# Four pieces of sample attention in place of eight, and the page loads spread along them

## The chip, the core and the metric

The kernel runs on one core of a Trainium2 chip. The metric is the device time of one execution in microseconds (us), the median of several runs. Engines are named as the profile names them: PE is TensorE's matmul, PEld its weight load, DVE is VectorE, ACT is ScalarE, POOL is GpSimd, SP is SyncE, which here issues every DMA.

## What is computed

One inference step of a decoder of two layers, in fp32, on 256 new prompt tokens and on 8 sample tokens, each sample with 256 cached tokens in two pages of 128. Cut to layer 2, which the change is in:

```
q, k, v, z = split(x @ w_in_attn)            # x: 256 prompt rows and 8 sample rows, width 1024
q, k = rope(q), rope(k)                      # first 32 of each head's 128 columns
prompt:  causal attention of 8 heads over the 256 rows
sample:  rows_k = cache_k[page_table], rows_v = cache_v[page_table]   # 2 pages a sample
         p = softmax(concat(q . rows_k, q . k_new) / sqrt(128))
         o = p @ concat(rows_v, v_new)
y = (o * silu(z)) @ w_out_attn
x = layernorm(sqrt(2) * x + y)
```

Layer 1 is a gated short convolution with projections of the same sizes.

## The kernel before

**Slabs.** Activations lie transposed: 8 blocks of 128 features by 264 columns (256 prompt, 8 sample). Each weight matrix is cut into slabs of 128 output features, numbered 0 to 79; slab 40+i is called "slab i" of layer 2 here, i from 0 to 31 (queries 0 to 7, keys 8 to 15, values 16 to 23, gate 24 to 31). A slab is 512 KB. Every weight is used as a high and a low part: ACT makes `hi` (L113), DVE makes `lo` (L118), and PE runs three matmuls for each of 8 blocks, 24 a slab (L125 to L127, "the stream").

**Order.** The program is written as a table of hooks: `at(n, phase, f)` puts a step in slab n, `begin(n)` runs the phases "dma", "pe", "s0", "hi", "lo", "s1a", "s1b", "s1" and so on in this order, and "peh" runs between a slab's first 12 and last 12 matmuls. Nothing is reordered later: each engine works its own list in order. SP issues the load of a slab's raw weights only behind the `lo` that frees one of four buffers (L116 to L118, then `load`), and the page loads `kv_load` stand in the same list, in phase "dma" of the slab that `KV_AT` names.

**Samples on cached pages.** 32 page tiles of 512 KB (16 of keys, two DMAs each, L242; 16 of values, one DMA each, L245) share 10 buffers `kv`; the first 10 are loaded in layer 1. `qk(step)`, steps 0 to 3, multiplies the samples' queries with four key tiles (16 matmuls, L690, into `sd`); `pvd(step)`, steps 4 to 7, the probabilities with four value tiles (8 matmuls, L742, into `dps`). The chip's trace shows each fp32 matmul as two. `QK_AT` and `PV_AT` name the slabs of these eight pieces. Tile i+10 takes the buffer of tile i, so its load waits for the piece that reads tile i.

**Around it.** PE's results lie in three rotating `acc` buffers; `k_evac` (ACT, L566 and L568) frees them in slabs 9 to 16, phase "s0". Prompt attention of head h: `s_mm` (PE, L622, L623) at the start of slab 16+h, `s_max` (DVE, L631 to L634), `s_exp` (ACT, L640), `s_norm` (DVE, L645, L647), `p_tr` and `v_tr` (PE, L653, L612) in the middle of slab 17+h. `s_mm`, `p_tr`, `v_tr` and `pv` take turns on three `att` buffers. `rope` (DVE, L577 to L580) for the last four key heads stands in slab 16, behind `s_norm` of head 0. After the last piece `od_copy`, `od_tr`, `os_fin` and `g_batch` make the samples' output and gate it; blocks that `g_batch` leaves out get it in `z_evac` by a copy on POOL (L776).

Of the kernel before, what the change touches and what calls it, by code (L numbers as in the profile page):

```python
# [38 lines left out]
C_COS = C_MASK + 128  # L39
C_SIN = C_COS + N  # L40
C_END = C_SIN + N
QK_AT = (6, 7, 10, 11)
KV_AT = (7, 7, 8, 8, 9, 9, 10, 11, 12, 13, 14, 15, 16, 17, 18, 19, 21, 21, 22, 22, 23, 24)
PV_AT = (21, 22, 24, 26)
SWAP = [(j + 16) % 32 for j in range(32)]


def build(tc, a):
    nc = tc.nc
    pe, act, dve, pool, sp = nc.tensor, nc.scalar, nc.vector, nc.gpsimd, nc.sync  # L50

    with ExitStack() as top:
# [79 lines left out]
        def at(n, phase, f, *args):  # L132
            hooks.setdefault((n, phase), []).append(lambda: f(*args))
# [371 lines left out]
        with tc.tile_pool(name="l1", bufs=1) as p1, ExitStack() as late_pool:  # L505
# [301 lines left out]
            S = 40  # L807
# [16 lines left out]
            at(S + 1, "s1", sd_fill)  # L824
            for i, n in enumerate(QK_AT):
                at(S + n, "peh", qk, i)
# [5 lines left out]
            at(S + 20, "s1a", pd_cp)  # L832
            for i, n in zip(range(NKV, 32), KV_AT):
                at(S + n, "dma", kv_load, i // 4, i % 4)
            for i, n in enumerate(PV_AT):
                at(S + n, "pe", pvd, 4 + i)
            at(S + 26, "s1", od_copy)
            at(S + 27, "pe", od_tr)
            at(S + 27, "s1", os_fin)
            at(S + 28, "s1", g_batch, 4)  # L840

            for h in range(8):
                n = S + 16 + h
# [180 lines left out]
```

## Time and profile before

| | |
|---|---|
| runs | 293.76, 291.53, 289.59 us; median 291.53 |
| the profiled execution's own time | 292.53 us |
| its span (first to last instruction) | 290.8 us |
| PE busy | 278.4 us, 96% |
| DVE, ACT, POOL busy | 186.0, 170.0, 62.8 us |
| DMA | 64.01 MB, mean 220 GB/s |

A busy PE is not yet a PE that does useful work at its full pace: its share counts overlapping matmuls. So the place where time is lost is read from the distances between the starts of matmuls, and from what ended PE's idle times. The chain of waits follows the end of the program back, at each step to what released it.

### The profile page before, as it was taken

How to read it: one execution, taken by the hardware profiler on the slowest of the kernel's cores; microseconds unless marked ns; L12 is line 12 of the kernel's file. 1: busy time of each engine (PE TensorE's matmuls, PEld its weight loads, DVE VectorE, ACT ScalarE, POOL GpSimd, SP SyncE). 2: the span in 40 equal slices, each digit the busy share in tenths (PEclk: the TensorE clock that was granted, in tenths of full speed). 3: DMA queues.
4: the chain of work that ended last, by engine and by line, in shares of the span. 5: the costliest groups of instructions: out<-in, count | busy, mean ns of one | idle time of the engine just before them, and what ended most of it. 6: DMA issues, size and time to landing. Idle time of an engine off the chain costs nothing.

```text
span 290.8 us, 6250 instructions
## 1 busy us (share of the span) xinstructions
PE 278.4 (96%) x2345; PEld 261.8 (90%) x2345; DVE 186.0 (64%) x347; ACT 170.0 (58%) x328; POOL 62.8 (22%) x120
## 2 busy tenths in 40 slices
PE   7999999999999999999999999979999999999980
PEld 4999999999999999999979699879779879999970
DVE  2957967465759759659985466796447147746144
ACT  4766655455366556355946399978557535553133
POOL 3110212021010108919420000000000003005643
PEclk9999999999999999999999999999999999999996
DMA  6985979999666763422069997979696643520003
GB/s 196 378 280 180 320 249 338 402 382 381 221 205 235 244 219 129 149 74 73 0 192 323 404 405 275 377 240 321 195 327 195 233 144 96 194 74 1 2 0 149
DMA packets 23215, 64.01 MB, mean 220 GB/s; under 512 B 2834, under 2 KB 5394, under 8 KB 23186
## 3 DMA queue, kind: packets, MB, share of 16 engines
q1 hardware_dynamic: 23186, 63.63, 62.8%
q8 instruction: 18, 0.29, 0.4%
q14 instruction: 11, 0.09, 0.1%
HBM read 60.30 MB, written 3.32 MB: 219 GB/s over the span
## 4 chain that ended last, share of the span: by engine, by line
PE 81%; ACT 7%; DMA 6%; DVE 3%; issue 1%; SPq 1%; DVEq 0%; ACTq 0%
PE acc L125 22%; PE acc L127 22%; PE acc L126 22%; DMA raw<-w 4%; PE dps L742 3%; ACT hi L113 3%; DMA kv<-kc 2%; PE sd L690 1%; PE acc L448 1%; PE o L662 1%; PE acc L449 1%; PE acc L452 1%; PE s L623 1%; PE pt L653 1%; ACT rp L568 1%
## 5 line engine op out<-in xcount | busy, mean ns | idle before, releaser
L118 DVE TENSOR_TENSOR lo<-raw,hi 128x1024 fp32r<-128x1024 f32 (+1 forms) x82 | 98.1, 1204 | 14.2 <-ACT hi L113 13.9
L113 ACT CAST hi<-raw 128x1024 fp32r<-128x1024 f32 (+1 forms) x82 | 82.9, 1017 | 38.8 <-DMA raw<-w 24.4
L125 PE MATMUL acc<-m0h,hi 128*128 128x264 f32 (+1 forms) x344 | 97.6, 284 | 0.0
L127 PE MATMUL acc<-m0h,lo 128*128 128x264 f32 (+1 forms) x344 | 97.5, 283 | 0.0
L126 PE MATMUL acc<-m0l,hi 128*128 128x264 f32 (+1 forms) x344 | 97.4, 283 | 0.0
L125 PE MATMUL acc<-m1h,hi 128*128 128x264 f32 x264 | 76.8, 291 | 0.0
L127 PE MATMUL acc<-m1h,lo 128*128 128x264 f32 x264 | 74.7, 283 | 0.0
L126 PE MATMUL acc<-m1l,hi 128*128 128x264 f32 x264 | 74.6, 283 | 0.0
L125 PEld LDWEIGHTS acc<-m0h,hi 128*128 128x128 f32 x344 | 64.7, 188 | 0.8 <-issue 0.4
L127 PEld LDWEIGHTS acc<-m0h,lo 128*128 128x128 f32 x344 | 64.9, 189 | 0.0
L126 PEld LDWEIGHTS acc<-m0l,hi 128*128 128x128 f32 x344 | 64.7, 188 | 0.0
L125 PEld LDWEIGHTS acc<-m1h,hi 128*128 128x128 f32 x264 | 49.7, 188 | 2.2 <-issue 2.1
L126 PEld LDWEIGHTS acc<-m1l,hi 128*128 128x128 f32 x264 | 49.7, 188 | 0.1
L127 PEld LDWEIGHTS acc<-m1h,lo 128*128 128x128 f32 x264 | 49.7, 188 | 0.0
L404 POOL COPY uo<-up 128x10 f32<-128x10 f32 x8 | 8.0, 1003 | 70.7 <-DVE up L403 62.4
L279 ACT ACTIVATE sqm<-xf 128x264 f32<-128x264 f32 x14 | 5.8, 423 | 20.1 <-DVE xf L259 20.1
L259 DVE SCALAR_TENSOR_TENSOR xf<-xf,acc 128x264 f32<-128x264 f32 x16 | 6.6, 425 | 12.4 <-PE acc L266 10.6
L287 POOL TENSOR_TENSOR q<-q,sqm 128x264 f32<-128x264 f32 x12 | 13.1, 1089 | 1.6 <-ACT sqm L279 1.5
L782 DVE TENSOR_TENSOR gt<-z,q 128x256 f32<-128x256 f32 (+1 forms) x8 | 3.4, 430 | 13.6 <-ACT z L773 13.6
L631 DVE TENSOR_TENSOR s<-s,cst 128x256 f32<-128x256 f32 x8 | 3.4, 431 | 12.3 <-PE s L623 12.3
L602 POOL COPY vs<-vh 128x8 f32<-128x8 f32 x8 | 1.6, 204 | 39.6 <-ACT vh L601 39.6
L286 POOL TENSOR_TENSOR sr<-sr,xf 128x264 f32<-128x264 f32 x10 | 9.3, 928 | 2.3 <-DVE xf L259 2.3
(187 smaller groups left out, 341.8 us busy)
## 6 DMA issues: line engine op xcount, KB each, us to landing
raw<-w SPq DMA_DIRECT2D x76, 512.0 KB, 4.7
kv<-kc SPq DMA_DIRECT2D x32, 256.0 KB, 6.1
kv<-vc SPq DMA_DIRECT2D x16, 512.0 KB, 5.4
raw<-w SPq DMA_DIRECT2D x7, 256.0 KB, 5.8
k_o<-k SPq DMA_DIRECT2D x8, 132.0 KB, 5.0
v_o<-vh SPq DMA_DIRECT2D x8, 132.0 KB, 4.5
y_o<-xf SPq DMA_DIRECT2D x4, 264.0 KB, 2.1
xf<-x SPq DMA_DIRECT2D x3, 264.0 KB, 5.8
```

The source lines that it names most:

```text
L113: act.copy(his[n][sl], raws[n][sl])
L118: dve.tensor_sub(los[n][sl], raws[n][sl], his[n].bitcast(F32)[sl])
L125: pe.matmul(acc, wh, mh[:, k, 0:w], start=first and k == ks[0], stop=False)
L126: pe.matmul(acc, wh, ml[:, k, 0:w], start=False, stop=False)
L127: pe.matmul(acc, wl, mh[:, k, 0:w], start=False, stop=last and k == ks[-1])
L259: dve.scalar_tensor_tensor(x, x, ALPHA, acc, ALU.mult, ALU.add)
L279: act.activation(self.last_sq, xf[:, m], AF.Square)
L286: pool.tensor_tensor(self.sr, self.sr, xf[:, m], ALU.add)
L287: pool.tensor_tensor(self.q, self.q, self.last_sq, ALU.add)
L404: pool.tensor_copy(uo[:, f], up[:, T:N + 2])
L631: dve.tensor_tensor(diag, diag, mask, ALU.add)
L742: pe.matmul(dps[0][32 * j:32 * j + 32, 512 * c:512 * c + 512], pm[b2][pg][:, j, :], kv_tiles[step, j][:, 512 * c:512 * c + 512], start=ste ...
```

## The change

The keys' pieces (`qk`) move from slabs 6, 7, 10, 11 to 7, 7, 14, 14; the values' pieces (`pvd`) from 21, 22, 24, 26 to 22, 22, 27, 27. The 22 page loads of layer 2 stand in other slabs: the first six were two a slab in slabs 7, 8 and 9, and are now two in slab 8 and one each in 9, 10, 11 and 12. The steps behind the last piece stand two slabs later, and the samples' gating takes six blocks in one batch, not four.

```
-QK_AT = (6, 7, 10, 11)
-KV_AT = (7, 7, 8, 8, 9, 9, 10, 11, 12, 13, 14, 15, 16, 17, 18, 19, 21, 21, 22, 22, 23, 24)
-PV_AT = (21, 22, 24, 26)
+QK_AT = (7, 7, 14, 14)
+KV_AT = (8, 8, 9, 10, 11, 12, 13, 14, 15, 15, 16, 17, 18, 19, 20, 21, 23, 23, 24, 24, 25, 25)
+PV_AT = (22, 22, 27, 27)
...
-            at(S + 26, "s1", od_copy)
-            at(S + 27, "pe", od_tr)
-            at(S + 27, "s1", os_fin)
-            at(S + 28, "s1", g_batch, 4)
+            at(S + 28, "s0", od_copy)
+            at(S + 29, "pe", od_tr)
+            at(S + 29, "s1", os_fin)
+            at(S + 30, "s1", g_batch, 6)
```

The first place is SP's list in slabs 6 to 10. `raw52` is slab 12's weights (40 + 12), `kv2_2` the key tile of step 2 and sample pair 2; of a tile's two DMAs one row is shown, and the rows that read a page's number are left out. Before:

```order
L103 DMA raw52_2178<-w 128x1024
L242 DMA kv2_2_2221<-kc 128x512
L242 DMA kv2_3_2224<-kc 128x512
L103 DMA raw53_2238<-w 128x1024
L242 DMA kv3_0_2281<-kc 128x512
L242 DMA kv3_1_2284<-kc 128x512
L103 DMA raw54_2295<-w 128x1024
L242 DMA kv3_2_2331<-kc 128x512
L242 DMA kv3_3_2334<-kc 128x512
L103 DMA raw55_2347<-w 128x1024
L103 DMA raw56_2351<-w 128x1024
L245 DMA kv4_0_2380<-vc 128x1024
```

Now:

```order
L103 DMA raw52_2178<-w 128x1024
L103 DMA raw53_2216<-w 128x1024
L242 DMA kv2_2_2275<-kc 128x512
L242 DMA kv2_3_2278<-kc 128x512
L103 DMA raw54_2289<-w 128x1024
L242 DMA kv3_0_2325<-kc 128x512
L103 DMA raw55_2338<-w 128x1024
L103 DMA raw56_2342<-w 128x1024
L242 DMA kv3_1_2371<-kc 128x512
L103 DMA raw57_2381<-w 128x1024
L103 DMA raw58_2385<-w 128x1024
L242 DMA kv3_2_2420<-kc 128x512
```

Of these page tiles none stands ahead of `raw53`, where there were two, two ahead of `raw54` in place of four, and three ahead of `raw55` in place of six.

The second place is PE's list around the first keys' piece, which was in the middle of slab 6 (weights `hi46`, `lo46`); `kv0_0` to `kv0_3` are the tiles of step 0. Before, the last matmul of the stream ahead of the piece, the piece's first four and the stream's next behind its 16:

```order
L127 MATMUL acc_2180<-m0h_89,lo46_1915 128x266
L690 MATMUL sd_1911<-kv0_0_755,zq_2017 16x256
L690 MATMUL sd_1911<-kv0_1_795,zq_2017 16x256
L690 MATMUL sd_1911<-kv0_2_830,zq_2017 16x256
L690 MATMUL sd_1911<-kv0_3_876,zq_2017 16x256
L125 MATMUL acc_2180<-m0h_89,hi46_1913 128x266
```

Now the last four matmuls of step 0 and the first four of step 1, in the middle of slab 7:

```order
L690 MATMUL sd_1911<-kv0_0_755,zq_2017 16x256
L690 MATMUL sd_1911<-kv0_1_795,zq_2017 16x256
L690 MATMUL sd_1911<-kv0_2_830,zq_2017 16x256
L690 MATMUL sd_1911<-kv0_3_876,zq_2017 16x256
L690 MATMUL sd_1911<-kv1_0_911,zq_2017 16x256
L690 MATMUL sd_1911<-kv1_1_951,zq_2017 16x256
L690 MATMUL sd_1911<-kv1_2_986,zq_2017 16x256
L690 MATMUL sd_1911<-kv1_3_1032,zq_2017 16x256
```

Step 1 now follows step 0 with no matmul of the stream between them.

## Rows read from the trace of the kernel before

**Rows 1.** The page: busy time, share and count of each engine.

```profile
PE 278.4 (96%) x2345; PEld 261.8 (90%) x2345; DVE 186.0 (64%) x347; ACT 170.0 (58%) x328; POOL 62.8 (22%) x120
```

**Rows 2.** Timeline of PE around the keys' piece of slab 6, then the first and the last of 65 matmuls of the undisturbed stream: start in us, duration, engine, line, what it does.

```profile
144.11 0.29 PE L127 MATMUL acc<-m0h,lo 128*128 128x266 f32 x1
144.32 1.92 PE L690 MATMUL sd<-kv,zq 128*16 128x256 f32 x32
146.18 0.39 PE L125 MATMUL acc<-m0h,hi 128*128 128x266 f32 x1
146.40 0.29 PE L126 MATMUL acc<-m0l,hi 128*128 128x266 f32 x1
...
152.11 0.28 PE L126 MATMUL acc<-m1l,hi 128*128 128x264 f32 x1
...
159.82 0.28 PE L127 MATMUL acc<-m1h,lo 128*128 128x264 f32 x1
```

**Rows 3.** Timeline of PE around the values' piece of slab 21, and around the same `s_mm` one slab earlier, where no piece stands ahead of it.

```profile
201.59 0.39 PE L622 MATMUL s<-k,q 128*128 128x128 f32 x2
201.81 0.60 PE L623 MATMUL s<-k,q 128*128 128x256 f32 x2
...
206.24 0.28 PE L127 MATMUL acc<-m1h,lo 128*128 128x264 f32 x1
206.45 1.92 PE L742 MATMUL dps<-kv,pm 128*32 128x512 f32 x16
208.31 0.49 PE L622 MATMUL s<-k,q 128*128 128x128 f32 x2
208.63 0.60 PE L623 MATMUL s<-k,q 128*128 128x256 f32 x2
```

**Rows 4.** Waits of PE by what ended them: us in total, times, longest.

```profile
PE s L622 <- ACT P L640: 1.5, 1, 1.5
PE pt L653 <- DVE P L647: 0.6, 1, 0.6
```

**Rows 5.** Timeline of PE around the keys' piece of slab 11; in brackets the idle time ahead of an instruction and what ended it.

```profile
164.98 0.62 PE L690 MATMUL sd<-kv,zq 128*16 128x256 f32 x6
166.12 1.89 PE L690 MATMUL sd<-kv,zq 128*16 128x256 f32 x26 [0.52 <-DMA kv<-kc]
167.93 0.39 PE L125 MATMUL acc<-m1h,hi 128*128 128x264 f32 x1
```

**Rows 6.** Timeline of PE: end of the stream's first half in slab 17, and `p_tr` of head 0.

```profile
186.58 0.28 PE L127 MATMUL acc<-m1h,lo 128*128 128x264 f32 x1
187.43 0.70 PE L653 MATMUL pt<-cst,P 128*128 128x128 f32 x3 [0.56 <-DVE P L647]
```

**Rows 7.** The chain of waits from 152.5 to 195 us: start, us, what.

```profile
153.42 6.12 DMA kv<-kc
159.61 7.67 DMA raw<-w
...
186.03 0.82 ACT P L640 x4
...
191.52 0.49 PE s L622 x2
```

**Rows 8.** Timeline of ACT in slabs 9 to 11, with the idle time ahead of an instruction; L566 is `k_evac`.

```profile
158.26 1.05 ACT L113 CAST hi<-raw 128x1024 fp32r<-128x1024 f32 x1 [1.67 <-DMA raw<-w]
162.27 1.06 ACT L113 CAST hi<-raw 128x1024 fp32r<-128x1024 f32 x1 [2.97 <-DMA raw<-w]
...
167.35 1.05 ACT L113 CAST hi<-raw 128x1024 fp32r<-128x1024 f32 x1 [2.36 <-DMA raw<-w]
...
169.16 0.38 ACT L566 COPY k<-acc 128x264 f32<-128x264 f32 x1
169.57 0.37 ACT L568 COPY rp<-acc 32x264 f32<-32x264 f32 x1
```

**Rows 9.** Busy time of each engine from 165 to 168 us, granted clock, DMA share and GB/s.

```profile
165.00:168.00 3.00, 2.48 (x34) 1.04 (x33) 1.21 (x3) 0.65 (x1) 0.00 (x0) 1.00 1.02 408
```

**Rows 10.** The page, DMA issues of whole weight slabs: count, KB each, median us from issue to landing.

```profile
raw<-w SPq DMA_DIRECT2D x76, 512.0 KB, 4.7
```

**Rows 11.** Timeline of DVE in slabs 16 and 17, between `s_max` of head 0 and `s_max` of head 1.

```profile
181.91 0.43 DVE L631 TENSOR_TENSOR s<-s,cst 128x256 f32<-128x256 f32 x1 [1.19 <-PE s L623]
...
183.59 1.23 DVE L118 TENSOR_TENSOR lo<-raw,hi 128x1024 fp32r<-128x1024 f32 x1 [0.39 <-ACT hi L113]
...
186.88 0.17 DVE L645 RECIPROCAL mx<-mx 128x2 f32<-128x2 f32 x1 [0.79 <-ACT P L640]
...
190.35 0.17 DVE L634 TENSOR_SCALAR mx<-mx 128x2 f32<-128x2 f32 x1
```

**Rows 12.** The kernel's two ends: timeline of PE from its first matmuls on, and the last stretch by windows (columns as in rows 9; 0.50 is the granted clock).

```profile
0.78 3.57 PE L75 MATMUL warmp<-const-bfloat16-1.0 128*128 128x512 bf16 x8 [0.78 <-PEq L1006]
...
4.67 0.42 PE L448 MATMUL acc<-m0h,w 128*128 128x264 f32 x1
4.89 0.42 PE L449 MATMUL acc<-m0l,w 128*128 128x264 f32 x1
...
7.65 0.28 PE L449 MATMUL acc<-m0l,w 128*128 128x264 f32 x1
...
286.00:290.80 4.80, 0.00 (x0) 0.00 (x0) 1.16 (x3) 0.53 (x2) 0.22 (x1) 0.50 0.57 219
```

## The prediction, made before the changed kernel ran

> **What bounds the kernel now.** I read the page first: PE is busy for 96% of the span [rows 1]. With so full an engine a change can gain only where the starts of its matmuls lie farther apart than the stream's own pitch. That pitch is (159.82 - 152.11) / 64 = 0.1205 us [rows 2], so 24 matmuls, a slab, take 2.9 us. Then I listed PE's waits and, because a wait of a pipelined engine is longer than its idle time, measured each in the timeline. In the stretch of the change there are three: a page that is late in slab 11 [rows 5], `p_tr` in slab 17 and `s_mm` in slab 18 [rows 4]. Last I followed the chain of waits back from that `s_mm`, to see whether the three have one cause.
>
> They mostly do. The chain runs from `s_mm` at 191.52 to ACT's exponential, through ACT's list back to a `hi` at 167.35 [rows 8], from there to a weight load issued at 159.61 that took 7.67 us, and to a page load ahead of it that took 6.12 us [rows 7]. The queue is full there: 408 GB/s [rows 9], by which a tile or slab of 512 KB [rows 10] takes 524,288 / 408e9 = 1.29 us. In slabs 7, 8 and 9 SP issues two page tiles and a weight slab each (slab 9 two weight slabs), 3.9 to 5.2 us of transfer for a slab of 2.9 us (4.9 with a piece in it). So ACT waits three times for weights, 1.67 + 2.97 + 2.36 = 7.00 us [rows 8], and because it works in order, everything behind those `hi` is late until the first heads of prompt attention want it.
>
> **The change, part by part.**
>
> *Four joins.* Entering a keys' piece costs more than the piece. From the stream's 144.11 to the piece is 0.21 us where a pitch is 0.12, and from the first matmul behind it to the next 0.22 [rows 2]: 0.09 + 0.10 = 0.19 us a piece beside its 1.86. A values' piece that is followed by `s_mm` pays the same: 0.21 us from 206.24 to 206.45, and 0.32 between the two forms of `s_mm` where it is 0.22 without a piece [rows 3]. Eight pieces become four double ones, so four entries go: 4 x 0.19 = 0.76 us. The work in the pieces is unchanged. If the seam between two pieces costs as much as an entry, this is 0; it can't be much more than 0.76.
>
> *The late page.* The piece of slab 11 lasts from 164.98 to 167.93, 2.95 us, where the undisturbed one takes 1.86 [rows 2, 5]: 1.09 us lost. Its last tiles were loaded in slab 9. Now the last key tile is loaded in slab 12 for slab 14, again two slabs ahead, but behind a queue with one page a slab: a page and a weight slab are 2.58 us of transfer for 2.90 us of stream, so the queue drains where it used to grow; and step 2's 1.86 us run ahead of the last tiles. I take the whole 1.09; the other end is 0.
>
> *The attention's start.* `p_tr` of head 0 starts 0.85 us behind the last matmul ahead of it, at a pitch of 0.12: 0.73 us lost; `s_mm` of head 2 waits another 1.5 us [rows 4, 6]. What sets the second is DVE's list between the row maxima of heads 0 and 1 [rows 11]: it waits 0.39 us for a `hi` and 0.79 us for the exponential of head 0, both because ACT is late. The rest, `lo`, the samples' key rotation, `s_norm`, `rope`, is work in a fixed order and stays. The double piece of slab 14 gives ACT 3.7 us more before slab 16, so it should arrive there in time. DVE then ends its list 0.39 + 0.79 = 1.18 us sooner, and `s_mm` of head 2 starts 1.18 us sooner: that is the gain, and not 0.73 + 1.5, since PE, let go at `p_tr`, waits longer at `s_mm`. About 1.5 us of that wait remains. Ends: 0 if ACT is as late as now, 1.18 + 1.5 if DVE should not be what it waits for.
>
> *What is moved at the end.* The last pages are issued in slab 25 for the second half of a double piece in slab 27. By then two tiles a slab in slabs 23 to 25 and a weight slab each make 9 x 1.29 = 11.6 us of transfer; slabs 23 to 26 last at least 206.45 - 201.59 = 4.86 us, for one with a head's attention and no piece [rows 3], and 3 x 2.9 for the others, 13.6 us, and the last four tiles are wanted another 1.86 us later. Cost 0, cover 2 to 4 us; without it PE would wait one for one. `od_copy` now stands ahead of `z_evac` on DVE and ACT in slab 28; three `acc` buffers give that evacuation two slabs. `g_batch` ends in slab 30 or early 31, and its columns are first read in the output projection, in slab 32. DVE does in slabs 29 and 30 what it did in 27 and 28, and no wait of PE came from there [rows 4]. Two POOL copies of 8 columns go: 0, POOL is not waited for.
>
> *The sum.* 0.76 + 1.09 + 1.18 = 3.03 us. The profiled execution took 292.53 us and would take 289.5; it lies 1.0 us above the median of the runs shown, 291.53, from which the same sum gives **288.5 us**.
>
> **Rivals.**
>
> *The jam only moves.* Pieces in slabs 10 and 11 held PE for 2.05 + 3.14 us in the old order, and this was ACT's time to catch up. Now slabs 8 to 13 are bare stream. `k_evac` at 169.16 to 169.94 [rows 8] frees the buffer that slab 13 needs; in the old order slab 13 began at 167.93 + 1.5 + 2.9 = 172.3, and without both pieces it would begin at 167.1. If weights come as late as now, PE waits there 2.8 us, and 288.5 + 2.8 gives 291.3: no change. Against it: ACT's 7.00 us came from the weights of slabs 13 to 15, and now none of the moved pages stands ahead of the first of them and half as many ahead of the other two. The Trainium skill speaks for this rival: "DMA: Bandwidth & Descriptors", Specifications, limits one core's traffic with HBM to about 358 GB/s. By that figure a page and a weight slab would be an estimated 2.93 us a slab, and the queue would never drain. The trace disagrees: 408 GB/s [rows 9]. Chance, from ACT's waits alone: 0.14.
>
> *A page is late again* in slab 14 or 27, as in slab 11 now: the 1.09 stay, 289.6. Chance 0.10.
>
> *DVE's list is not the limit*, and the 1.5 us at `s_mm` go as well: 287.0. For it: the wait is put down to ACT [rows 4]. Against: head 1's maximum ends at 190.52 [rows 11], and from there to `s_mm` at 191.52 is 1.0 us, hardly more than one head's exponential of 0.82 [rows 7]. Chance 0.10.
>
> *The clock falls in a double piece*, which makes the kernel slower. For 3.7 us PE then does only narrow fp32 matmuls of 16 or 32 columns. At the granted clock's lower level, 0.50 or 1.2 GHz, matmuls of 264 columns start 0.22 us apart, as at the kernel's beginning; there PE began at 0.78, was still at that level at 4.89 and at the higher one, by the durations, at 7.65 [rows 12]. So a low stretch that long, 4.1 to 6.9 us, loses 1 - 0.12 / 0.22 = 45% of itself, 1.9 to 3.1 us; I take 2.5. One fall gives 291.0, two 293.5, and from two on the kernel is slower. Against: the clock is granted in full in the window that holds the piece of slab 11 with its wait [rows 9], and at the end it is low only after the last matmul [rows 12]. Chance 0.04, at 293.5.
>
> **The numbers.** The forecast has 0.62, with its own range of 287.3 to 289.8 (the seam's price, half a wait more or less, and a median of runs that spread from 289.59 to 293.76). The range over all cases, 286.4 to 291.2, takes in 287.0 and 289.6 and most of what lies below the first rival's 291.3. Faster by over 2% (under 285.7 us) would need more than all three waits: 0.05. Slower by over 2% (over 297.4) needs all four double pieces to lose the clock, or an unseen wait: 0.02. Within 2%, about what a measurement of this kernel can tell from no change: 0.93.
>
> **What would show it.** Right: keys' pieces of 3.7 us with only one entry each; no wait for pages; ACT's waits for weights in slabs 8 to 11 well under 7.00 us; `p_tr` of head 0 not late; `s_mm` of head 2 still waiting about 1.5 us, and DVE's list from maximum to maximum without waits. Wrong: PE waiting for an `acc` buffer in slabs 12 to 14, for `kv` in slab 14 or 27, or for `odt` in slab 29; a granted clock under 1.00 inside layer 2.

## The result, and the profile of the changed kernel

The changed kernel took **288.63 us** in the median (seven runs of 288.09 to 288.99; an eighth, at a granted clock of 0.70, took 488.88 and is not counted), the kernel before 291.5 in the runs beside it (289.59 to 293.76). The ratio is 0.9894, with a 95% interval of 0.9866 to 0.9923: a real gain of about 1%, within the 2% that count as no change here. The forecast was 288.5. The profiled execution of the changed kernel took 288.65 us, its span is 286.9.

The page of the changed kernel: busy times, the granted clock in 40 slices, and the chain that ended last.

```profile
PE 275.0 (96%) x2345; PEld 261.2 (91%) x2345; DVE 185.5 (65%) x347; ACT 169.4 (59%) x328; POOL 64.8 (23%) x120
...
PEclk9999999999999999999999999999999999999997
...
PE 91%; DVE 3%; DMA 2%; ACT 1%; SPq 0%; issue 0%; DVEq 0%; ACTq 0%
```

The chain of the kernel before:

```profile
PE 81%; ACT 7%; DMA 6%; DVE 3%; issue 1%; SPq 1%; DVEq 0%; ACTq 0%
```

PE's share is 96% as before [rows 1], with 3.4 us less of it, so the share tells nothing of the gain. The chain does: 91% of it is PE's own work now, where it was 81%, and ACT and DMA hold 3% together, where they held 13%. The granted clock is 0.9 of full or more in every slice but the last (the digits are tenths).

Its waits of PE (us in total, times, longest), against [rows 4, 5]:

```profile
PE acc L448 <- ACT w L113: 2.0, 1, 2.0
PE s L622 <- ACT P L640: 1.0, 1, 1.0
```

The waits for `kv` and at `p_tr` are gone, that at `s_mm` of head 2 is 1.0 where it was 1.5. The first line lies in the kernel's first 10 us, outside the change.

Timeline of PE in the changed kernel: a matmul at the seam of the two layers (L266), the two keys' pieces, `s_mm` of head 0 (179.35), the matmul ahead of `s_mm` of head 2 (L702, `own_mm`) and that `s_mm`, and the last matmul of the program.

```profile
107.92 0.28 PE L266 MATMUL ln<-s,ones 128*128 128x264 f32 x1
...
147.08 0.28 PE L127 MATMUL acc<-m1h,lo 128*128 128x264 f32 x1
147.29 3.65 PE L690 MATMUL sd<-kv,zq 128*16 128x256 f32 x64
150.87 0.39 PE L125 MATMUL acc<-m1h,hi 128*128 128x264 f32 x1
151.09 0.29 PE L126 MATMUL acc<-m1l,hi 128*128 128x264 f32 x1
...
171.32 3.65 PE L690 MATMUL sd<-kv,zq 128*16 128x256 f32 x64
...
179.35 0.38 PE L622 MATMUL s<-k,q 128*128 128x128 f32 x2
...
187.00 0.28 PE L702 MATMUL sd<-onesf,pr 128*128 128x1 f32 x2
188.27 0.49 PE L622 MATMUL s<-k,q 128*128 128x128 f32 x2 [0.99 <-ACT P L640]
...
278.14 1.00 PE L329 MATMUL lnb<-st,sel 128*128 128x66 f32 x8
```

And three rows of the same kind for the kernel before:

```profile
107.88 0.28 PE L266 MATMUL ln<-s,ones 128*128 128x264 f32 x1
...
181.06 0.38 PE L622 MATMUL s<-k,q 128*128 128x128 f32 x2
...
282.02 1.00 PE L329 MATMUL lnb<-st,sel 128*128 128x66 f32 x8
```

From the first of these matmuls to the end of the last, layer 2 takes 278.14 + 1.00 - 107.92 = 171.22 us, where it took 282.02 + 1.00 - 107.88 = 175.14: 3.92 us less, the whole difference of the spans (290.8 - 286.9). "Length of layer 2" below is this distance; it leaves out what the first layer does from run to run. From `s_mm` of head 0 to that of head 2 it is 188.27 - 179.35 = 8.92 us, where it was 191.52 - 181.06 = 10.46 [rows 7]: 1.54 us less. A double keys' piece holds PE from 147.29 to 150.87, 3.58 us, where two single ones took 2 x 1.86 [rows 2].

Windows that hold the first keys' and the first values' double piece (columns as in [rows 9]): the granted clock in them is 1.00.

```profile
147.30:150.90 3.60, 3.60 (x66) 1.79 (x65) 3.53 (x7) 2.29 (x3) 1.79 (x2) 1.00 0.64 225
...
207.90:211.50 3.60, 3.60 (x34) 0.94 (x32) 0.00 (x0) 1.42 (x2) 0.19 (x1) 1.00 0.56 204
```

Timeline of ACT in the changed kernel, against [rows 8]: the only `hi` that waits for weights between 152 and 192 us, the `k_evac` of slab 13's output, and the last `k_evac`, of slab 15's.

```profile
158.81 1.05 ACT L113 CAST hi<-raw 128x1024 fp32r<-128x1024 f32 x1 [1.54 <-DMA raw<-w]
...
171.83 0.36 ACT L566 COPY k<-acc 128x264 f32<-128x264 f32 x1
...
179.55 0.38 ACT L566 COPY k<-acc 128x264 f32<-128x264 f32 x1 [0.31 <-PE acc L127]
```

ACT waits 1.54 us for weights where it waited 7.00, and at its last two `k_evac` it waits for PE (0.65 and 0.31 us): it is ahead of PE, where before it was late. Timeline of DVE, from the maximum of head 0 to that of head 1, in the changed kernel (against [rows 11]):

```profile
181.34 0.17 DVE L634 TENSOR_SCALAR mx<-mx 128x2 f32<-128x2 f32 x1
181.41 1.23 DVE L118 TENSOR_TENSOR lo<-raw,hi 128x1024 fp32r<-128x1024 f32 x1
...
182.57 0.21 DVE L590 STREAM_SHUFFLE qsr<-ks 32x64 f32<-32x64 f32 x1
...
183.40 0.34 DVE L699 TENSOR_TENSOR pr<-qs,ks 128x32 f32<-128x32 f32 x2
183.65 0.16 DVE L645 RECIPROCAL mx<-mx 128x2 f32<-128x2 f32 x1
...
187.10 0.17 DVE L634 TENSOR_SCALAR mx<-mx 128x2 f32<-128x2 f32 x1
```

No row of it carries a wait. `s_mm` of head 2 follows the end of this list by 188.27 - 187.10 = 1.17 us, as it did before (191.52 - 190.35 [rows 7, 11]).

### The profile page after: what moved, and what is told of

Its sections match the earlier page's. It is cut to its first block, busy times and chain, and to the rows that moved or that the text cites. A ratio compares the mean times of both kernels' runs of the same rounds, so it can differ in the third digit from the quotient of the medians.

```text
span 286.9 us, 6246 instructions
## 1 busy us (share of the span) xinstructions
PE 275.0 (96%) x2345; PEld 261.2 (91%) x2345; DVE 185.5 (65%) x347; ACT 169.4 (59%) x328; POOL 64.8 (23%) x120
## 4 chain that ended last, share of the span: by engine, by line
PE 91%; DVE 3%; DMA 2%; ACT 1%; SPq 0%; issue 0%; DVEq 0%; ACTq 0%
PE acc L125 25%; PE acc L127 25%; PE acc L126 25%; PE sd L690 2%; PE dps L742 2%; DMA raw<-w 2%; PE acc L448 1%; PE o L662 1%; PE acc L449 1%; PE acc L452 1%; PE s L623 1%; PE pt L653 1%; DVE xf L929 1%; PE lnb L329 1%; PE s L622 1%; PE o L663 1%
```

## The experiments

Each is the changed kernel with the lines shown, or the kernel before with them where that is said; none leaves out computation. The table gives what was read from all of them; "weights" is ACT's wait for weights between 152 and 192 us, "0 to 2" the distance from `s_mm` of head 0 to that of head 2 (none where a piece stands between). In three runs (before again, pages two a slab, keys in 11) the profile puts one wait of a `hi`, 1.25 to 1.29 us, down to `rope` on DVE; it is counted as a wait for weights here, since each of these `hi` starts 0.07 or 0.08 us behind a landing of weights, as the other waiting ones do (0.02 to 0.08), and 0.00 to 0.04 behind the end of `rope`. The kernel before ran beside them at 292.01 to 292.04 us.

| kernel | median us | ratio to before, 95% | layer 2 us | weights us | 0 to 2 us |
|---|---|---|---|---|---|
| before, as shown ahead | 291.5 | 1 | 175.14 | 7.0 | 10.46 |
| before again | 291.37, one run | none | 174.13 | 6.0 | 10.46 |
| changed | 288.63 | 0.9894 [0.9866, 0.9923] | 171.22 | 1.5 | 8.92 |
| changed again | 288.84 | 0.9895 [0.9865, 0.9925] | 171.22 | 2.4 | 8.92 |
| keys only | 289.48 | 0.9915 [0.9885, 0.9944] | 171.83 | 2.4 | 8.91 |
| values only | 291.23 | 0.9974 [0.9948, 1.0] | 173.57 | 6.1 | 10.60 |
| unjoined | 289.90 | 0.9924 [0.9899, 0.995] | 172.78 | 2.5 | 8.90 |
| pages two a slab | 288.79 | 0.9908 [0.9876, 0.9941] | 171.21 | 3.0 | 8.90 |
| six pages at once | 293.49 | 1.0049 [1.0015, 1.0082] | 176.10 | 7.3 | 8.90 |
| keys in 11 | 290.46 | 0.9937 [0.9903, 0.997] | 173.33 | 6.2 | 10.49 |
| rope on POOL | 287.65 | 0.9847 [0.9812, 0.9883] | 170.36 | 2.2 | 8.05 |
| rope on POOL again | 287.97 | 0.9851 [0.9819, 0.9884] | 170.35 | 2.5 | 8.04 |
| keys in 16 | 287.41 | 0.9845 [0.9805, 0.9885] | 170.05 | 2.4 | none |

### Both kernels again

The kernel before once more, one execution:

> The kernel before once more, for its trace. In the values-only run the page wait of slab 11 was absent. If that wait comes and goes with the state of the DMA queue, it may be absent here too, and the waits at p_tr and s_mm (0.7 and 1.5 us) should stay, since they come from ScalarE's lateness of 6 to 7 us. Rival, the page wait belongs to this order of the pieces: 1.1 us again.

Timeline of PE in it: first and last matmul as above, and the piece of slab 11, which in the trace before lasted 2.95 us [rows 5].

```profile
107.72 0.28 PE L266 MATMUL ln<-s,ones 128*128 128x264 f32 x1
...
164.83 2.01 PE L690 MATMUL sd<-kv,zq 128*16 128x256 f32 x32
166.77 0.39 PE L125 MATMUL acc<-m1h,hi 128*128 128x264 f32 x1
...
280.85 1.00 PE L329 MATMUL lnb<-st,sel 128*128 128x66 f32 x8
```

Here the piece takes 1.94 us, and layer 2 takes 174.13, 1.01 less than in the other trace of the same kernel, and matmul by matmul the two differ nowhere else in it. So the late page of slab 11 comes and goes, and 1.0 us of layer 2 with it. The attention's start is late in both: 10.46 us from `s_mm` of head 0 to that of head 2.

The changed kernel:

> The changed kernel on the same chip as the next one. All theories: 2.5 to 3.9 us under the kernel before, no page wait, s_mm of head 2 waiting about 1.0 us.

It repeats to 0.01 us in layer 2 and 0.2 us in the median.

### The keys' half and the values' half alone

The kernel before, with the keys' pieces and their pages alone moved, and then the changed kernel with the keys' side put back:

```
# keys only, from the kernel before
-QK_AT = (6, 7, 10, 11)
-KV_AT = (7, 7, 8, 8, 9, 9, 10, 11, 12, 13, 14, 15, 16, 17, 18, 19, 21, 21, 22, 22, 23, 24)
+QK_AT = (7, 7, 14, 14)
+KV_AT = (8, 8, 9, 10, 11, 12, 13, 14, 15, 15, 16, 17, 18, 19, 20, 21, 21, 21, 22, 22, 23, 24)
# values only, from the changed kernel
-QK_AT = (7, 7, 14, 14)
-KV_AT = (8, 8, 9, 10, 11, 12, 13, 14, 15, 15, 16, 17, 18, 19, 20, 21, 23, 23, 24, 24, 25, 25)
+QK_AT = (6, 7, 10, 11)
+KV_AT = (7, 7, 8, 8, 9, 9, 10, 11, 12, 13, 14, 15, 16, 17, 18, 19, 23, 23, 24, 24, 25, 25)
```

> Only the keys' half of the change: pieces in slabs 7, 7, 14, 14 and the first sixteen page loads spread as changed; values' pieces, the steps behind them and the batch of four as before. My theory (two joins at about 0.33 us each, the late page 1.1, DVE's waits between the first two maxima 1.2 to 1.5): PE waits for no page, ACT's waits for weights in slabs 8 to 11 under 2 us, and the time is 2.9 to 3.3 us under the kernel before in the trace. Rival, the values' half brings a good part of the gain: only about 1.5 to 2 us under. Rival, joins are worth nothing: 2.2 to 2.6 us under.

> Only the values' half: pieces in 22, 22, 27, 27 with their loads, the later steps and the batch of six; keys' pieces and their loads as before. My theory: two joins, 0.6 to 0.7 us under the kernel before; the page wait of about 1.1 us in slab 11 and the waits at p_tr in slab 17 and s_mm in slab 18 stay. Rival, the values' half brings a good part of the gain: 1.5 to 2 us. Rival, joins are worth nothing: 0.

Against the second trace of the kernel before (174.13) the keys' half takes 2.30 us from layer 2, the values' half 0.56; both together took 2.91. (The 2.9 to 3.3 us expected of the keys' half had counted the late page, and its ACT waits 2.4 us for weights, not under 2.) The keys' half has the changed kernel's 8.91 us at the attention's start and no wait at `p_tr`; its profiled execution lost the clock for a while in layer 1, so layer 2 is the better measure. The values' half keeps the old waits at `p_tr` (0.7) and `s_mm` (1.5). It has no late page in slab 11, against what was expected: with the old keys' side the page is late in one of three traces.

### The pieces apart again

```
-QK_AT = (7, 7, 14, 14)
-PV_AT = (22, 22, 27, 27)
+QK_AT = (7, 8, 14, 15)
+PV_AT = (22, 23, 27, 28)
```

> The changed kernel with each double piece taken apart by one slab: keys in 7, 8, 14, 15, values in 22, 23, 27, 28; page loads and all else as changed. My theory: eight entries again, so 4 x 0.33 = 1.3 us over the changed kernel in the trace, each piece lasting 1.85 us and no new waits. The prediction's price of an entry alone, without a gain at the seam: 0.76 us over. Rival, what counts is only the page loads' order: 0.

Timeline of PE around the keys' piece of slab 7:

```profile
147.14 0.28 PE L127 MATMUL acc<-m1h,lo 128*128 128x264 f32 x1
147.35 1.92 PE L690 MATMUL sd<-kv,zq 128*16 128x256 f32 x32
149.20 0.39 PE L125 MATMUL acc<-m1h,hi 128*128 128x264 f32 x1
149.43 0.29 PE L126 MATMUL acc<-m1l,hi 128*128 128x264 f32 x1
```

From the stream's last matmul ahead of the piece to its second behind it, a single piece takes 149.43 - 147.14 = 2.29 us, and a double one 151.09 - 147.08 = 4.01. Two pitches of 0.12 of the stream are in each, so two single pieces cost 2 x (2.29 - 0.24) = 4.10, the double one 3.77: **0.33 us for a join**, not 0.19. Both parts are in the rows: 0.19 at the two edges, as read before, and 2 x 1.86 - 3.58 = 0.14 between a piece's first matmul and the stream's next, once a piece however long it is. The single records, which the rows merge, show where most of the 0.14 lies: inside a piece the narrow matmuls come in fours, 0.20 us from one four to the next, also at the seam of two pieces, and from the last narrow one to the stream's next it is 0.31. So it belongs to the way out. Summed over the four pairs in the same way, apart costs 1.29 us. Layer 2 grew by 172.78 - 171.22 = 1.56; the other 0.27 us come in the layernorm that ends the program, where DVE's first step on the sums (L307) waits 1.38 us for PE in place of 1.03. Why it does is open. In the output projection nothing is lost, and PE waits for nothing there, though the last piece stands a slab later. The joins do not touch the attention's start: 8.90.

The Trainium skill has a rule on this, in "TensorEngine Tiling (Array Packing)", Tiling Modes, Key Properties: changing the tiling mode drains TensorE, and changing only the tile within a mode does not. The trace agrees as far as it goes: a seam between two pieces of the same narrow form costs nothing that shows, while each way in and out of them costs 0.33 us in all. That it is a drain, no row shows.

### The pages two a slab, and six at once

The forecast had two reasons for ACT being on time: the pages spread over slabs 8 to 12, and the double piece in slab 14. These runs take the first away, and leave the second. (The pages' numbers behind the first six are as in the changed kernel.)

```
-KV_AT = (8, 8, 9, 10, 11, 12, ...
+KV_AT = (8, 8, 9, 9, 10, 10, ...     # pages two a slab
+KV_AT = (8, 8, 8, 8, 8, 8, ...       # six pages at once
```

> The changed kernel with the first six page loads two a slab again, in slabs 8, 8, 9, 9, 10, 10 (all joined pieces as changed). The prediction's first rival made real: if weights behind bunched pages come late, ScalarE waits 5 to 7 us for them in slabs 9 to 12, frees an accumulator too late for the bare stream of slabs 12 and 13, and PE waits there 1 to 3 us: slower than the changed kernel by as much. My theory in its weaker form: the wait for weights grows to 4 to 6 us but the accumulators' cover holds, and the double piece of slab 14 lets ScalarE catch up: within 0.5 us of the changed kernel. Rival, loads' order means nothing: ScalarE's wait stays at 1.5 us.

> The changed kernel with its first six page loads all in slab 8, ahead of the weights of slab 14. It makes weights late on purpose. If the double piece of slab 14 is what puts ScalarE back on time before the first head: ScalarE waits 4 to 8 us for weights in slabs 9 to 11, but p_tr of head 0 does not wait and s_mm of head 2 waits about 1.0 us as in the changed kernel; PE loses 0 to 3 us for an accumulator in slabs 12 or 13. Rival, lateness of weights alone decides: p_tr waits 0.7 us again and s_mm 1.5 us.

Two a slab, as in the kernel before but one slab later, costs nothing: 171.21 us of layer 2. ACT waits 1.74 us for weights, and then 1.25 in this row, which is put down to `rope`; weights landed at 162.46, and `rope` ended at 162.54:

```profile
162.54 1.05 ACT L113 CAST hi<-raw 128x1024 fp32r<-128x1024 f32 x1 [1.25 <-DVE rp L580]
```

Six at once costs 4.88 us. Timeline of ACT in that run, the `hi` of the slab behind the jam and the last `k_evac`; then the timeline of PE around its wait; then windows of one microsecond (length, busy time of PE, PEld, DVE, ACT and POOL with counts, granted clock, DMA share, GB/s):

```profile
164.84 1.04 ACT L113 CAST hi<-raw 128x1024 fp32r<-128x1024 f32 x1 [7.29 <-DMA raw<-w]
...
184.74 0.38 ACT L566 COPY k<-acc 128x264 f32<-128x264 f32 x1 [0.24 <-PE acc L127]
```

```profile
164.17 0.28 PE L127 MATMUL acc<-m1h,lo 128*128 128x264 f32 x1
167.60 0.59 PE L125 MATMUL acc<-m1h,hi 128*128 128x264 f32 x1 [3.15 <-ACT rp L568]
...
170.85 0.30 PE L127 MATMUL acc<-m1h,lo 128*128 128x264 f32 x1
```

```profile
163.00:164.00 1.00, 1.00 (x11) 1.00 (x10) 0.00 (x0) 0.00 (x0) 0.00 (x0) 1.00 1.06 422
...
168.00:169.00 1.00, 1.00 (x6) 1.00 (x6) 0.96 (x3) 0.99 (x3) 0.00 (x0) 0.50 0.83 205
```

This is the first rival's mechanism, made to happen: weights behind pages, ACT late, PE out of `acc` buffers in the slabs of bare stream. PE loses 167.60 - 164.17 - 0.12 = 3.31 us of starts, and behind the wait the clock is at its lower level until 170.85: 14 matmuls take 170.85 - 167.60 = 3.25 us where they take 14 x 0.1205 = 1.69, another 1.56. That is the 4.88, and more than the 0 to 3 us expected, which had no clock in it. Yet for the attention nothing is left of ACT's lateness: it waits for PE again at its last `k_evac`, and the attention's start takes the same 8.90. How late ACT is can be read from `k_evac`: its start less that of the last matmul of the slab that it empties. Here that is 172.87 - 164.17 = 8.70 us for slab 11, 3.53 for slab 12, once PE has waited, 2.99 for slab 13, and 0.32 for slab 15, behind the double piece. So PE's own wait, with the low clock behind it, took off most of what the jam had brought, and the double piece the rest.

### The double piece in slab 11

The counter-test: the second double piece ahead of slab 14, with its pages early enough for it.

```
-QK_AT = (7, 7, 14, 14)
-KV_AT = (8, 8, 9, 10, 11, 12, ...
+QK_AT = (7, 7, 11, 11)
+KV_AT = (8, 8, 8, 8, 9, 9, ...
```

> The changed kernel with the second double keys' piece in slab 11 in place of 14, so its pages are loaded in slabs 8, 8, 8, 8, 9, 9. No piece stands between slab 11 and the first head. If the place of the double piece decides (it gives ScalarE 3.6 us when it is late): ScalarE is 2 to 3 us late at slab 16, p_tr waits 0.5 to 0.8 us and s_mm of head 2 about 1.5 us: 1.0 to 1.6 us over the changed kernel, more if a page is late. Rival, joining and fewer pages ahead of the weights is enough: within 0.3 us of the changed kernel.

PE's waits in this run, and ACT's for weights from 152 to 192 us:

```profile
PE s L622 <- ACT P L640: 1.5, 1, 1.5
...
PE pt L653 <- DVE P L647: 0.6, 1, 0.6
```

```profile
ACT hi L113 <- DMA raw<-w: 4.9, 1, 4.9
```

Both old waits are back at their old size, and the start of the attention takes 10.49 us. That alone would fit bunched pages too: ACT waits 4.9 us for weights, 6.2 with the wait put down to `rope`. What tells the two reasons apart is how late `k_evac` is, read as above, on either side of slab 14:

| kernel | slab 13 us | slab 15 us |
|---|---|---|
| before | 2.48 | 3.27 |
| changed | 2.16 | 0.32 |
| pages two a slab | 3.65 | 0.65 |
| six pages at once | 2.99 | 0.32 |
| keys in 11 | 2.50 | 3.28 |
| keys in 16 (below) | 3.00 | 3.78 |

In the changed kernel the first is 171.83 - 169.67. ACT comes to slab 14 late in all six, with spread pages (2.16, 3.00) about as much as in the kernel before, and is on time behind it, or nearly, only where a double piece stands in it. "Keys in 16" has the changed kernel's pages up to slab 14 and no piece between slabs 7 and 16, and ACT is 3.78 us late. So it is the place of the piece, right ahead of the attention, that gives the 1.54 us; how the pages are spread does not. The rest of this run's 2.11 us over the changed kernel is a page: its piece in slab 11 takes 4.14 us, 0.56 over 3.58.

### What the attention's start still waits for

The forecast held that DVE's list sets the start of `s_mm` of head 2, and left 1.5 us of that wait standing. If so, a shorter list must shorten it; if ACT's exponentials set it, nothing comes of it. The last key heads' `rope` goes to POOL, its shuffle stays:

```
-                dve.tensor_mul(r, r, cos)
-                dve.tensor_mul(s, s, sin)
-                dve.tensor_add(r, r, s)
+                e = pool if (w, q4) == (1, 1) else dve
+                e.tensor_tensor(r, r, cos, ALU.mult)
+                e.tensor_tensor(s, s, sin, ALU.mult)
+                e.tensor_tensor(r, r, s, ALU.add)
```

> The changed kernel with the two products and the sum of one of four rope calls (last four key heads, in slab 16) on GpSimd in place of VectorE. If VectorE's list between the maxima of heads 0 and 1 sets the start of s_mm of head 2 (the prediction): that list gets 1.2 to 1.3 us shorter, the remaining wait of about 1.0 us there goes, and the time falls by 0.9 to 1.2 us against the changed kernel. Rival, ScalarE's exponential is late for its own list: no change. Rival, GpSimd is too slow (some 1.1 us an operation): ScalarE's copy of key head 4 in slab 18 comes late, and PE waits in slab 20: slower by 0.5 to 2 us.

> The kernel with one rope call's products and sum on GpSimd, beside the changed kernel on one chip. If VectorE's list is what s_mm of head 2 waits for: 0.8 to 1.2 us under the changed kernel, in the trace 0.86 us less between own_mm and s_mm. Rival, the first comparison was between two chips and the gain is less: 0 to 0.4 us.

Timeline of PE in the first of the two (lines from L577 on stand one lower; L703 is `own_mm`, L623 `s_mm` of head 2), and the last row of DVE's list, the maximum of head 1:

```profile
187.05 0.28 PE L703 MATMUL sd<-onesf,pr 128*128 128x1 f32 x2
187.46 0.49 PE L623 MATMUL s<-k,q 128*128 128x128 f32 x2
```

```profile
185.84 0.61 DVE L635 TENSOR_SCALAR mx<-mx 128x2 f32<-128x2 f32 x1
```

From `own_mm` to `s_mm` it is 0.41 us, in the changed kernel 1.27: 0.86 us less, and no wait is listed. Layer 2 shows the same 0.86, and the repeat 0.87. DVE's list from maximum to maximum is 185.84 - 181.38 = 4.46 us long where it was 5.76, so 1.30 shorter; but its last row takes 0.61 us where it took 0.17, in both traces, beside a product on POOL (185.67 to 186.43). So 0.44 us of the gain are lost there; that POOL is the cause is not shown. The list is the limit.

The other way to use this is to cover the list instead of shortening it: the double piece goes where PE would otherwise wait for it.

```
-QK_AT = (7, 7, 14, 14)
-KV_AT = (8, 8, 9, 10, 11, 12, 13, 14, 15, 15, 16, 17, 18, 19, 20, 21, 23, 23, 24, 24, 25, 25)
+QK_AT = (7, 7, 16, 16)
+KV_AT = (8, 8, 9, 10, 11, 12, 13, 14, 17, 17, 18, 18, 19, 20, 21, 21, 23, 23, 24, 24, 25, 25)
```

> The changed kernel with the second double keys' piece in the middle of slab 16, behind s_mm of head 0, and eight later page loads moved by up to two slabs. PE then does 3.6 us of sample work while VectorE goes through its list from the first maximum to the second: if that list is what s_mm of head 2 waits for, its wait of 1.0 us goes, 0.8 to 1.0 us under the changed kernel, even though ScalarE comes to slab 16 late by 2 to 3 us. Rival, ScalarE's lateness at slab 16 comes back as waits at p_tr or later heads: 0 to 1.5 us over the changed kernel.

Timeline of PE in this run: `s_mm` of head 0, the double piece, `own_mm`, `s_mm` of head 2.

```profile
175.49 0.38 PE L622 MATMUL s<-k,q 128*128 128x128 f32 x2
...
177.68 3.65 PE L690 MATMUL sd<-kv,zq 128*16 128x256 f32 x64
...
186.92 0.28 PE L702 MATMUL sd<-onesf,pr 128*128 128x1 f32 x2
187.06 0.47 PE L622 MATMUL s<-k,q 128*128 128x128 f32 x2
```

`s_mm` follows `own_mm` by 0.14 us and waits for nothing. Layer 2 takes 170.05 us, 1.17 less than in the changed kernel, of which 1.27 - 0.14 = 1.13 is this wait. ACT's lateness at slab 16 does not come back as a wait of PE; the `k_evac` of slab 15's output, whose last matmul starts one pitch ahead of `s_mm` of head 0, at 175.37:

```profile
179.15 0.36 ACT L566 COPY k<-acc 128x264 f32<-128x264 f32 x1
```

With 287.41 us it has the lowest median of all kernels here, though the two intervals of its ratio and of rope on POOL overlap almost wholly.

## Why the prediction was right

The mechanism of the main term held, but all three terms had another size: two were too small, by 0.53 and 0.36 us, and one was 1.01 too large. These errors cancel to 0.12, and that the time came out so near (288.63 for 288.5) is luck.

- **The attention's start**, forecast 1.18 us: right in its cause, small in its size. DVE's list lost both of its waits, and `s_mm` of head 2 starts sooner by what the list lost, 1.54. The 1.18 was the sum of the two idle times in brackets, 0.39 + 0.79 [rows 11]. The forecast had said itself that a wait of a pipelined engine is not its idle time, and measured PE's by starts, but took DVE's from the brackets. Here are the rows of the kernel before that stand ahead of and behind those two:

```profile
183.03 0.17 DVE L634 TENSOR_SCALAR mx<-mx 128x2 f32<-128x2 f32 x1
...
184.91 0.21 DVE L590 STREAM_SHUFFLE qsr<-ks 32x64 f32<-32x64 f32 x1
...
185.74 0.35 DVE L699 TENSOR_TENSOR pr<-qs,ks 128x32 f32<-128x32 f32 x2
```

  By starts, maximum to `lo` took 183.59 - 183.03 = 0.56 and takes 0.07 now; `lo` to the shuffle 1.32, now 1.16; `pr` to the reciprocal 186.88 - 185.74 = 1.14, now 0.25. That is 0.49 + 0.16 + 0.89 = 1.54.
- **The four joins**, forecast 0.76 us: mis-sized. "It can't be much more than 0.76" was wrong, since the edges were counted as far as the pitch shows them, and the 0.14 us on the way out was taken for work of the piece. A join gives 0.33 by the rows, and the four measured 1.29 where they were undone.
- **The late page**, forecast 1.09 us: a wait of one execution, not of the kernel. The trace that the sum was made against had it; the second trace has 1.94 - 1.86 = 0.08 of it. Measured against that second trace the terms are 1.29 + 1.54 + 0.08 = 2.91, and layer 2 lost 174.13 - 171.22 = 2.91; the forecast's sum was 3.03. The profiled execution before lay 1.0 us above its median, so much of this term should not have been taken from a median as well. That the executions without a profile mostly lack the late page is argued from this, and not shown.
- **The reasons for ACT being on time**: the double piece of slab 14 is the cause, by the runs above. That half as many pages stand ahead of the weights, which the forecast set against the first rival, shows in the trace (1.5 us of waits for 7.0) but is worth nothing: ahead of slab 14 ACT is 2.16 or 3.00 us late with spread pages and 2.48 in the kernel before, and two pages a slab took the same time. So the jam of pages, to which the forecast mostly traced the three waits, is not what decides: with pages one a slab and no piece in slab 14 ACT is 3.78 us late at the attention's start, where it was 3.27.
- **The end**, forecast 0: right. No wait for `kv` in slab 27, none for `odt`; the values' double pieces last 3.57 us as the keys' do. With the last piece one slab later PE waits for none of these either.
- **The rivals.** The jam that only moves is a real mechanism, but came only with six pages at once; at one or two a slab PE waits for no `acc` buffer in slabs 12 to 14. Its price had been put at 2.8 us without the clock behind the wait. The limit of about 358 GB/s that spoke for it, from the Trainium skill ("DMA: Bandwidth & Descriptors", Specifications), does not bind here either: the queue moved 422 GB/s in the first window of the jam above. No page is late in slab 14 or 27. DVE's list is the limit, by rope on POOL and by keys in 16. The clock does not fall in the double pieces (1.00 in their windows); where it fell, behind the jam's wait, it cost 1.56 us, less than the 1.9 to 3.1 reckoned for a fall.
- **"About 1.5 us of that wait remains"**: 1.0 by the list of waits, 1.15 by starts (1.27 less a pitch), for the reason of the first point.

## What to carry to other kernels

A block of side work is not only something to hide or to join: while PE does it, the engines that prepare PE's operands catch up, so put it in one piece where they are late, or better where a chain of dependences would leave PE idle. Price the switch into and out of such a block by the starts on both sides, and by blocks of two lengths. Price a wait by starts too, on any engine that pipelines, DVE included, and not by the idle time in brackets. And look for a wait in a second trace before its whole length goes into a sum: here one of three was there in one execution and not in the next two.

## What the runs showed of the hardware

- A run of narrow matmuls has a cost of its own, beside the 0.19 us at its edges: 32 take 1.86 us and 64 take 3.58, so 1.72 / 32 = 0.054 us each and 0.14 us once, most of it on the way out.
- PE's granted clock was 1.00 through 3.58 us of matmuls of 16 or 32 columns, but was at 0.50 behind a wait of 3.3 us, where the wait itself was two thirds of what it cost: 3.31 of 4.88 us.
- Behind six page tiles issued together ACT waited 7.29 us for the next weights, where it waits 1.54; 20 us later ACT was on time again, but the 4.88 us that PE had lost were not won back.
